# Sums and low parts of activation quarters read from PSUM in the seven-product scheme of a SwiGLU down-projection (one Trainium2 core)

## The chip, the core and the metric

The kernel runs on 1 core of one Trainium2 chip. The metric is the device time of one execution in microseconds (us); times are medians of several executions unless a single profiled execution is named.

## What is computed

The reference is one inference step of a streaming encoder layer: 2048 prompt rows and 64 sample rows, model width 1024. After convolution and attention comes a gated feed-forward part, in which the change lies:

```python
h2 = rms_norm(x, norm2_g) * (1 + sc2) + sh2
gate, up = jnp.split(h2 @ w_ffn_in, 2, axis=-1)         # each 2816 wide
x = x + gt2 * ((jax.nn.silu(gate) * up) @ w_ffn_out)    # 2816 x 1024
```

Everything is float32.

## The kernel before, in words

**Precision.** A float32 product is made of three matmuls (`mm3`): each operand is split into a high part `hi` (type fp32r) and a low part `lo = x - hi`, and TensorE (PE) accumulates hi·hi, hi·lo and lo·hi in PSUM. For activations ScalarE (ACT) writes `hi` with a Copy and VectorE (DVE) or GpSimd (POOL) writes `lo` with a subtraction. For weights ACT writes `whi` and mostly POOL writes `wlo`. Five weight slabs of such parts are held at a time.

**Passes.** The last phase treats the 2112 rows in three passes `s` (`CBLOCKS`: 576, 768 and 768 rows). `half` is half of a pass's rows: 288 in the first, 384 in the other two. The 2816 hidden columns are 22 tiles `f` of 128.

**Gate and up.** `up(f, ...)` makes one hidden tile for both halves by seven products in place of eight (Strassen-Winograd): steps `s2`, `s3`, `s1`, `a12`, `a22`, `a11` of the next tile, and `s4`, each 12 matmuls into a PSUM bank of 384 columns. Banks come from two tags of four banks each: `y` (for the running products `y` and `z`) and `gp` (for `x` and for the down-projection's `pd`). The ends are: `z` times `c1` (silu of the gate, SBUF) is the hidden value of the first half of the rows, and `y` times `v` (SBUF) that of the second half.

**Down, in the second and third pass.** For tiles 4 to 19 (`PAIRS`, eight pairs `f, f+1` per pass, sixteen in all) the down-projection also takes seven products. The two tiles and the two row halves are the four quarters of the left operand: `A11` and `A21` from the even tile, `A12` and `A22` from the odd one. `paired` makes the sums S3 = A11 - A21, S2 = A22 - S3, S1 = S2 + A11 and S4 = A12 - S2, and `put` splits each of the seven operands A11, S3, A12, A22, S2, S1, S4 into `hi` and `lo` in an eighth of the tile `hid`. `low` asks the planner (`either`) whether DVE or POOL does the subtraction.

`down_pair(f, j)` runs while the next pair's `up` is under way, at four points: j=0 (products B21, T3), j=1 (T4, B11), j=2 (T2, T1) and j=3 (B22). Each product is three groups of three matmuls of 512 columns, one group per 128 rows, and after each group DVE adds the bank to a row accumulator in SBUF: `acc<-acc,pd`. Banks are short: T4 goes on in T3's banks, and T2, T1, B22 go on in B11's, so a group of T1 can start only when DVE has added the same bank's T2 group; and with four `gp` banks the last groups of T3 take banks that B21's groups have to leave first.

**Order.** The kernel's text is only one input to the order: the framework that builds the program gives every engine a fixed list of instructions. `Stream` is a planner inside the kernel that keeps a load figure for each engine; it decides which engine makes a low part and when weights are split. In the text, the two SBUF tiles of the pair (`c1`, `v`) receive the hidden values, and all sums and splits read and write SBUF (`paired`, lines 1817 to 1842; `up`, lines 1937 to 1952). S3, S2, S1 and S4 are written over `v`, `v`, `c1` and `c1`.

In the profile nearly all instructions stand under line 104, that of a recording helper, so tiles tell them apart: `hid<-v,hid` and `hid<-s,hid` are low parts of quarters in SBUF, `v<-v` is S2, `v<-s,v` S3, `s<-v,s` S1 and `s<-s,v` S4 (`s` is the buffer that holds `c1`), `wlo<-wst,whi` (or `wup`, `wfo`, `ws`) is the low part of weights.

Of the kernel before, what the change touches and what calls it, by code (L numbers as in the profile page):

```python
# [10 lines left out]
AF = mybir.ActivationFunctionType  # L11
ALU = mybir.AluOpType
# [67 lines left out]
def tile_chunks(lo, hi):  # L80

    tiles = token_tiles(lo, hi)
    t, n = tiles[(len(tiles) + 1) // 2 - 1]
    return [(lo, t + n), (t + n, hi)]
# [499 lines left out]
def streaming_layer(ctx: ExitStack, tc: tile.TileContext, I, O):  # L584
    nc = tc.nc
    stream = Stream()
    pe, dve, act, gps = (
        Meter(e, n, stream) for e, n in ((nc.tensor, "pe"), (nc.vector, "dve"), (nc.scalar, "act"), (nc.gpsimd, "pool"))
    )
# [88 lines left out]
    def split(hi, lo, src):  # L678
        act.activation(hi, src, AF.Copy)
        stream.after("dve", "act")  # L680
        dve.tensor_tensor(lo, src, hi.bitcast(F32), ALU.subtract)

    def either(n, less=0.0):

        d, p = (max(stream.load[e], stream.load["pe"]) for e in ("dve", "pool"))
        return (gps, "pool") if p + 60 + 2.25 * n + less < d + 75 + 1.04 * n else (dve, "dve")

    def low(hi, lo, src, n, less=0.0):
        e, name = either(n, less)
        stream.after(name, "act")  # L690
        e.tensor_tensor(lo, src, hi.bitcast(F32), ALU.subtract)
        return name
# [344 lines left out]
    def half_piece(i, name):  # L1037
        return (wc, wk)[i].tile([P, CW // 2], F32, tag=f"tg{i}", name=name, bufs=2 + i)
# [7 lines left out]
    def load_mixed(c0, c1, i):  # L1046

        src = [[quarter("cin", i) for _ in range(2)] for _ in range(2)]
        for j, a in enumerate((c_d, o_d)):
            for l in range(2):  # L1050
                nc.sync.dma_start(src[l][j][:, :, : c1 - c0].bitcast(F32), a[l, :, :, c0:c1].rearrange("c p t -> p c t"))
        return src
# [437 lines left out]
    for b, stage in ORDER:  # L1490
        lo, hi = PBLOCKS[b]
        if stage == "q":
            free, ahead = {"columns": 0}, {}
# [16 lines left out]
        elif stage == "g":  # L1510
            for g in gates(b, free):
# [3 lines left out]
                if g == SIDE_G and b == len(PBLOCKS) - 1:  # L1515
# [6 lines left out]
                    src = load_mixed(*cs, 0)  # L1522
                    first_gates = gate_columns(*cs, 0)
            norms = ahead
        else:
            if b == 0 and stage == 1:
                bias_rows()
            if stage == 0:
                conv.drain()
                tail.drain()  # L1530
                y = wk.tile([P, 4, YW], F32, tag="y", name="y")
# [33 lines left out]
    def piece(tag, name):  # L1565
        return wk.tile([P, CW // 2], F32, tag=tag, name=name, bufs={"t1": 2, "t2": 3}[tag])
# [117 lines left out]
    c0, c1 = tile_chunks(*CBLOCKS[0])  # L1684
# [3 lines left out]
    for s, (lo, hi) in enumerate(CBLOCKS):  # L1688
        tiles = token_tiles(lo, hi)
        half = (hi - lo) // 2  # L1690
# [58 lines left out]
        def product(ps, w, b, first, last):  # L1749

            for k in range(4):
                mm3(
                    ps[:, :half], w[0][:, k], w[1][:, k], hs[b][0][:, k, :half], hs[b][1][:, k, :half],
                    first and k == 0, last and k == 3, skip_group_check=True,
                )

        def bank(tag):
            return ps_g.tile([P, 512], F32, tag=tag, name="ps", bufs=4)[:, :half]
# [5 lines left out]
        def plus(dst, ps, b):  # L1764
            stream.after("dve", "pe", "act")
            dve.tensor_tensor(dst, ps, b, ALU.add)

        def silu(dst, z):

            tg = half_piece(0, "tg")[:, :half]  # L1770
            stream.after("act", "pe", "dve")
            act.activation(tg, z, AF.Tanh, scale=0.5)
            stream.after("dve", "act")
            dve.scalar_tensor_tensor(dst, tg, 1.0, z, ALU.add, ALU.mult)

        def slot(q):

            return hid[q % 8 // 4][:, q % 4]

        def whole(f, i):  # L1780

            return slot(2 * (f % 2) + i + 4 * (f >= NF - 2))
# [9 lines left out]
        def hidden(f, i, ps):  # L1792
            if s:
                hi, lo = (whole(f, i)[:, j] for j in range(2))
            else:
                hi, lo = (hid[f >= NF - 4 and f % 4 // 2][:, f % 2, j, i * half : (i + 1) * half] for j in range(2))
            stream.after("act", "dve")
            split(hi, lo, ps)

        def plain(f, i, ps):  # L1800
            hidden(f, i, ps)
            yield 1

        quad = {}

        def put(f, name, src):

            q = quad[f - f % 2]
            a = q["parts"][name] = slot(7 * (f // 2 - PAIRS.start // 2) + 4 + len(q["parts"]))
            stream.after("act", "dve")  # L1810
            act.activation(a[:, 0], src, AF.Copy)
            low(a[:, 0], a[:, 1], src, half)

        def minus(dst, x, y, e=ALU.subtract):
            dve.tensor_tensor(dst, x, y, e)

        def paired(f, i, src):

            q = quad.setdefault(f - f % 2, {"parts": {}})
            if f % 2 == 0:  # L1820
                if i == 0:
                    q["a11"] = src
                    put(f, "A11", src)
                else:
                    minus(src, q["a11"], src)
                    q["s3"] = src
                    put(f, "S3", src)
            elif i == 0:
                q["a12"] = src
                put(f, "A12", src)  # L1830
            else:
                put(f, "A22", src)
                yield 1
                s2, s1, s4 = q["s3"], q["a11"], q["a12"]
                minus(s2, src, s2)
                put(f, "S2", s2)
                minus(s1, s2, s1, ALU.add)
                put(f, "S1", s1)
                yield 1
                minus(s4, s4, s2)  # L1840
                put(f, "S4", s4)
            yield 1

        class Operands:
# [18 lines left out]
        begun, late = {}, []  # L1863
# [23 lines left out]
        def rest_of_late(n=99):  # L1887
            while late and n:
                n -= 1
                if next(late[0], None) is None:  # L1890
                    late.pop(0)

        def up(f, ops, at):
            def step(ps, op, b, first, last, e=f):
                product(ps, ops.use(e, op), b, first, last)
                ops.done()

            if f < EARLY:
                s1, c1 = (t[:, :half] for t in early[f])
                y = bank("y")  # L1900
            else:
                y, s1 = begun.pop(f)
                c1 = s1

            z = None
            if not f:
                z = bank("y")
                step(z, "s3", "t3", True, False)
            step(y, "s2", "t2", f < EARLY, False)
            rest_of_late(1)  # L1910
            u2 = piece("t1", "u2")[:, :half]
            keep = (lambda dst, ps: plus(dst, ps, s1)) if f < EARLY else copy
            keep(u2, y)
            if f % 2:
                at(3)
            if f:
                z = bank("y")
                step(z, "s3", "t3", True, False)
            v = half_piece(1, "v")[:, :half]
            keep(v, z)  # L1920
            rest_of_late()
            if f % 2 == 0:
                at(0)
            step(y, "s1", "t1", False, False)
            plus(v, y, v)
            if f % 2:
                at(4)
            if f >= EARLY:
                x = bank("gp")
                step(x, "a12", "b21", True, True)  # L1930
                plus(x, x, s1)
                silu(c1, x)
            if f % 2 == 0:
                at(1)
            step(z, "a22", "t4", False, True)
            plus(z, z, u2)
            two = s and f - f % 2 in PAIRS
            h = [c1, v] if two else [z, y]
            dve.tensor_tensor(h[0], z, c1, ALU.mult)
            if EARLY <= f + 1 < NF:  # L1940
                ny = bank("y")
                step(ny, "a11", "b11", True, False, f + 1)
                begun[f + 1] = ny, piece("t2", "s1")[:, :half]
                copy(begun[f + 1][1], ny)
            for _ in paired(f, 0, h[0]) if two else [hidden(f, 0, z)]:
                pass
            step(y, "s4", "b22", False, True)
            if f < EARLY:
                plus(y, y, s1)
            silu(y, y)  # L1950
            dve.tensor_tensor(h[1], y, v, ALU.mult)
            late.append(paired(f, 1, h[1]) if two else plain(f, 1, y))

        def down(fs, ws):

# [67 lines left out]
        for f in range(0, NF, 2):  # L2023
# [6 lines left out]
            def at(i, f=f):  # L2030
                if s and f - 2 in PAIRS:
                    if i in dn_at(f - 2):
                        down_pair(f - 2, dn_at(f - 2).index(i))
                elif i == 0 and 2 <= f <= NF - 4:
                    down([f - 2, f - 1], [W.get(("fo", e)) for e in (f - 2, f - 1)])
# [10 lines left out]
        for i, (t, n) in enumerate(tiles):  # L2046
            for j in range(2):
                q = 2 * i + j
# [35 lines left out]
```

## Time and profile before

| | |
|---|---|
| median of 3 runs | 3088.68 us (3081.73 to 3092.24) |
| the profiled execution | 3091.31 us, span of its instructions 3089.5 us |
| mean granted TensorE clock | 0.985 |
| PE busy | 2948.6 us (95% of the span) |
| DVE, ACT, POOL busy | 2092.8, 1233.9, 1005.2 us (68%, 40%, 33%) |
| bytes moved by DMA | 693.07 MB, 224 GB/s |

A row of the list of groups gives the operation as out<-in, the count, the busy time and the mean of one in ns, then the idle time of the engine before them and who ended it. A row of the time-ordered list gives start and duration in us; an idle time before it, with the instruction that ended the wait, stands in brackets.

### The profile page before, as it was taken

To read this page: it belongs to the slowest core of one execution; us is meant where nothing else is said; L and a number is where in the kernel's file an instruction comes from. 1 tells how busy PE (TensorE), PEld (TensorE's weight loads), DVE (VectorE), ACT (ScalarE), POOL (GpSimd) and SP (SyncE) were. 2 spreads that over 40 slices of the span, in tenths; PEclk is the share of its full clock that TensorE was granted. 3 is DMA by queue.
4 is the path that set the end of the run, shared out by engine and by line. 5 is a ranking of instruction groups with operands and counts; after the bars stand their busy time and mean duration, and the time that the engine had idled before them with its cause. 6 is when DMAs were issued, how large, how long until landed. Compare 5 with 4: busy or idle time off the path is not lost. (4 is left out here: it accounts for less than half of the span.)

```text
span 3089.5 us, 44838 instructions
## 1 busy us (share of the span) xinstructions
PE 2948.6 (95%) x16259; PEld 2611.9 (85%) x16259; DVE 2092.8 (68%) x3817; ACT 1233.9 (40%) x2212; POOL 1005.2 (33%) x626
## 2 busy tenths in 40 slices
PE   7989898999999999989999999999999999999998
PEld 4789777887888788888888889998888898989887
DVE  4797687777977885466666756556666757366667
ACT  2324431452255257454433345334434244333322
POOL 0200210101011102445666342265766341343341
PEclk9999998999999999999999999999999999999999
DMA  9788788888997798876444776445545955345444
GB/s 341 251 276 304 217 289 275 266 267 267 302 283 234 263 271 248 256 275 223 148 150 141 266 251 216 142 159 180 184 159 195 352 197 191 124 152 176 156 152 175
DMA packets 487082, 693.07 MB, mean 224 GB/s; under 512 B 38484, under 2 KB 316872, under 8 KB 486861
## 3 DMA queue, kind: packets, MB, share of 16 engines
q1 hardware_dynamic: 474581, 672.82, 66.4%
q10 hardware_dynamic: 12280, 17.39, 1.6%
q8 instruction: 128, 2.10, 0.3%
q14 instruction: 93, 0.76, 0.1%
HBM read 505.89 MB, written 184.19 MB: 223 GB/s over the span
## 5 line engine op out<-in xcount | busy, mean ns | idle before, releaser
L104 POOL TENSOR_TENSOR wlo<-wst,whi 128x1024 fp32r<-128x1024 f32 (+1 forms) x175 | 391.6, 2244 | 485.6 <-ACT whi L104 421.5
L104 PE MATMUL ps<-t,whi 128*128 128x384 f32 (+1 forms) x2112 | 503.4, 324 | 11.0 <-DVE t L104 4.8
L104 PE MATMUL pd<-whi,hid 128*128 128x512 f32 (+1 forms) x1400 | 455.1, 394 | 33.4 <-DVE acc L104 33.4
L104 ACT ACTIVATE whi<-wst 128x1024 fp32r<-128x1024 f32 (+1 forms) x269 | 261.8, 977 | 384.6 <-PE ps L104 97.1
L104 PE MATMUL ps<-b,whi 128*128 128x384 f32 (+1 forms) x1584 | 382.6, 327 | 10.8 <-DVE pw L104 4.0
L104 PEld LDWEIGHTS ps<-t,whi 128*128 128x128 f32 x2112 | 370.5, 189 | 20.2 <-DVE t L104 5.8
L104 DVE SCALAR_TENSOR_TENSOR y<-u,wd,y 128x512 f32<-128x512 f32 (+1 forms) x480 | 368.3, 771 | 6.5
L104 PE MATMUL ps<-hh,whi 128*128 128x512 f32 (+2 forms) x992 | 364.1, 367 | 0.0
L104 PE MATMUL ps<-hl,whi 128*128 128x512 f32 (+2 forms) x992 | 347.3, 350 | 0.0
L104 PE MATMUL ps<-hh,wlo 128*128 128x512 f32 (+2 forms) x992 | 346.7, 350 | 0.0
L104 PEld LDWEIGHTS pd<-whi,hid 128*128 128x128 f32 (+1 forms) x1400 | 258.2, 184 | 104.3 <-DVE acc L104 47.0
L104 PE MATMUL ps<-t,wlo 128*128 128x384 f32 (+1 forms) x1056 | 340.6, 323 | 0.0
L104 DVE TENSOR_TENSOR acc<-acc,pd 128x512 f32<-128x512 f32 (+1 forms) x440 | 285.3, 681 | 66.4 <-PE pd L104 62.8
L104 PEld LDWEIGHTS ps<-b,whi 128*128 128x128 f32 x1584 | 279.3, 190 | 14.1 <-DVE pw L104 4.3
L104 PE MATMUL pd<-wlo,hid 128*128 128x512 f32 (+1 forms) x700 | 274.1, 392 | 0.0
L104 PE MATMUL ps<-b,wlo 128*128 128x384 f32 (+1 forms) x792 | 257.9, 326 | 0.0
L104 POOL TENSOR_TENSOR r<-t,mhalf 128x8 f32<-128x8 f32 (+3 forms) x68 | 84.4, 1243 | 392.8 <-DVE t L104 369.4
L104 PEld LDWEIGHTS ps<-hh,wlo 128*128 128x128 f32 x992 | 188.3, 190 | 22.4
L104 PEld LDWEIGHTS ps<-hh,whi 128*128 128x128 f32 x992 | 189.1, 191 | 18.6 <-issue 2.1
L104 PEld LDWEIGHTS ps<-hl,whi 128*128 128x128 f32 x992 | 189.1, 191 | 15.4 <-issue 1.7
L104 POOL TENSOR_TENSOR wlo<-wup,whi 128x1024 fp32r<-128x1024 f32 (+1 forms) x62 | 133.9, 2160 | 208.7 <-ACT whi L104 202.4
L104 PEld LDWEIGHTS ps<-t,wlo 128*128 128x128 f32 x1056 | 199.2, 189 | 0.0
(231 smaller groups left out, 5794.2 us busy)
## 6 DMA issues: line engine op xcount, KB each, us to landing
whi<-w_din_h SPq DMA_DIRECT2D x72, 512.0 KB, 6.4
wlo<-w_din_l SPq DMA_DIRECT2D x72, 512.0 KB, 6.7
wst<-sum_d SPq DMA_DIRECT2D x131, 256.0 KB, 2.9
wmod<-in_w_ada SPq DMA_DIRECT2D x48, 512.0 KB, 8.0
sum_d<-ws SPq DMA_DIRECT2D x88, 256.0 KB, 2.2
wst<-in_w_ffn_in SPq DMA_DIRECT2D x85, 256.0 KB, 3.4
wst<-in_w_ffn_in SPq DMA_DIRECT2D x37, 512.0 KB, 5.3
wst<-in_w_in SPq DMA_DIRECT2D x36, 512.0 KB, 6.6
```

The source lines that it names most:

```text
L104: return f(*args, **kw)
```

## The change

The hidden values stay in their PSUM banks: `z` is overwritten with z·c1 and `y` with y·v. High parts, low parts and sums are taken from there, and the sums are written back into the bank, so each of DVE's subtractions and additions has one operand in PSUM and the other in SBUF. Low parts of quarters are always made by DVE (`split`). Three values that are needed again after their bank is overwritten, or as the second operand of a later sum, are copied to SBUF by ACT: A11 into `c1`, S3 into `v`, and S2 over S3 in `v`.

```diff
-        def put(f, name, src):
+        def put(f, name, ps):
 
             q = quad[f - f % 2]
             a = q["parts"][name] = slot(7 * (f // 2 - PAIRS.start // 2) + 4 + len(q["parts"]))
             stream.after("act", "dve")
-            act.activation(a[:, 0], src, AF.Copy)
-            low(a[:, 0], a[:, 1], src, half)
-
-        def minus(dst, x, y, e=ALU.subtract):
-            dve.tensor_tensor(dst, x, y, e)
-
-        def paired(f, i, src):
+            split(a[:, 0], a[:, 1], ps)
+
+        def paired(f, i, ps, free):
 
             q = quad.setdefault(f - f % 2, {"parts": {}})
-            if f % 2 == 0:
-                if i == 0:
-                    q["a11"] = src
-                    put(f, "A11", src)
-                else:
-                    minus(src, q["a11"], src)
-                    q["s3"] = src
-                    put(f, "S3", src)
+            if f % 2 == 0 and i == 0:
+                put(f, "A11", ps)
+                act.activation(free, ps, AF.Copy)
+                q["a11"] = free
+            elif f % 2 == 0:
+                dve.tensor_tensor(ps, q["a11"], ps, ALU.subtract)
+                put(f, "S3", ps)
+                act.activation(free, ps, AF.Copy)
+                q["s3"] = free
             elif i == 0:
-                q["a12"] = src
-                put(f, "A12", src)
+                put(f, "A12", ps)
+                q["a12"] = ps
             else:
-                put(f, "A22", src)
+                put(f, "A22", ps)
                 yield 1
-                s2, s1, s4 = q["s3"], q["a11"], q["a12"]
-                minus(s2, src, s2)
-                put(f, "S2", s2)
-                minus(s1, s2, s1, ALU.add)
-                put(f, "S1", s1)
+                z, keep = q["a12"], q["s3"]
+                dve.tensor_tensor(ps, ps, keep, ALU.subtract)
+                put(f, "S2", ps)
+                act.activation(keep, ps, AF.Copy)
+                dve.tensor_tensor(ps, ps, q["a11"], ALU.add)
+                put(f, "S1", ps)
                 yield 1
-                minus(s4, s4, s2)
-                put(f, "S4", s4)
+                stream.after("dve", "act")
+                dve.tensor_tensor(z, z, keep, ALU.subtract)
+                put(f, "S4", z)
             yield 1
...
             two = s and f - f % 2 in PAIRS
-            h = [c1, v] if two else [z, y]
-            dve.tensor_tensor(h[0], z, c1, ALU.mult)
+            dve.tensor_tensor(z, z, c1, ALU.mult)
...
-            for _ in paired(f, 0, h[0]) if two else [hidden(f, 0, z)]:
+            for _ in paired(f, 0, z, c1) if two else [hidden(f, 0, z)]:
...
-            dve.tensor_tensor(h[1], y, v, ALU.mult)
-            late.append(paired(f, 1, h[1]) if two else plain(f, 1, y))
+            dve.tensor_tensor(y, y, v, ALU.mult)
+            late.append(paired(f, 1, y, v) if two else plain(f, 1, y))
```

Over the program the change turns 112 low parts (96 on DVE, 16 on POOL) into 112 on DVE, adds 48 ACT copies, and, since the planner's figure for POOL is lower, moves 7 low parts of weights (128x1024) from DVE to POOL, all in the second pass.

What it does to the order is seen at two places of a pair in the second pass. **Place A** is j=2, when T2 and T1 are run: DVE's rows there from the silu of `y` in an even tile on. Before (S3 is `v<-s_21585,v`, its low part `hid<-v,hid`):

```order
L104 SCALAR_TENSOR_TENSOR ps<-tg,ps 128x384
L104 TENSOR_TENSOR v<-ps,v 128x384
L104 TENSOR_TENSOR v<-s_21585,v 128x384
L104 TENSOR_TENSOR acc<-acc,pd 128x512
L104 TENSOR_TENSOR hid<-v,hid 128x384
L104 TENSOR_TENSOR acc<-acc,pd 128x512 x5
L104 TENSOR_TENSOR v<-ps,v 128x384
```

The same place of the changed kernel (S3 is `ps<-s_21593,ps`):

```order
L104 SCALAR_TENSOR_TENSOR ps<-tg,ps 128x384
L104 TENSOR_TENSOR ps<-ps,v 128x384
L104 TENSOR_TENSOR ps<-s_21593,ps 128x384
L104 TENSOR_TENSOR acc<-acc,pd 128x512
L104 TENSOR_TENSOR hid<-ps,hid 128x384
L104 TENSOR_TENSOR acc<-acc,pd 128x512 x5
L104 TENSOR_TENSOR v<-ps,v 128x384
```

Nothing moved here: the same instruction stands between the first and the second addition, with other operands.

**Place B** is j=0, when B21 and T3 are run and S2, S1 and S4 are made, on DVE from the silu of `y` in the odd tile on. Before (`hid<-v,hid` is the low part of A22, then of S2; the low part of S1 is not in DVE's list here, POOL makes it; `hid<-s_21803,hid` is that of S4):

```order
L104 TENSOR_TENSOR v<-ps,v 128x384
L104 TENSOR_TENSOR v<-v 128x384
L104 TENSOR_TENSOR hid<-v,hid 128x384
L104 TENSOR_TENSOR s_21585<-v,s_21585 128x384
L104 TENSOR_TENSOR hid<-v,hid 128x384
L104 TENSOR_TENSOR s_21803<-s_21803,v 128x384
L104 TENSOR_TENSOR acc<-acc,pd 128x512
L104 TENSOR_TENSOR wlo<-wup,whi 128x1024
L104 TENSOR_TENSOR hid<-s_21803,hid 128x384
L104 TENSOR_TENSOR acc<-acc,pd 128x512 x5
L104 TENSOR_TENSOR v<-ps,v 128x384
```

The same place of the changed kernel, in the order low part of A22, S2, two additions, low part of S2, an addition, S1, S4, an addition, low parts of S1 and S4, two additions:

```order
L104 TENSOR_TENSOR ps<-ps,v 128x384
L104 TENSOR_TENSOR hid<-ps,hid 128x384
L104 TENSOR_TENSOR ps<-ps,v 128x384
L104 TENSOR_TENSOR acc<-acc,pd 128x512 x2
L104 TENSOR_TENSOR hid<-ps,hid 128x384
L104 TENSOR_TENSOR acc<-acc,pd 128x512
L104 TENSOR_TENSOR ps<-ps,s_21593 128x384
L104 TENSOR_TENSOR ps<-ps,v 128x384
L104 TENSOR_TENSOR acc<-acc,pd 128x512
L104 TENSOR_TENSOR hid<-ps,hid 128x384 x2
L104 TENSOR_TENSOR acc<-acc,pd 128x512 x2
L104 TENSOR_TENSOR v<-ps,v 128x384
```

Two additions now stand ahead of the rest of the chain where one stood behind it, and the weights' low part is gone from DVE's list. ACT at place B, before (`u` and `v` from `ps` are copies of running products, `hid` the high parts):

```order
L104 ACTIVATE u_22044<-ps 128x384
L104 ACTIVATE hid<-v 128x384 x2
L104 ACTIVATE whi<-wup 128x1024
L104 ACTIVATE v<-ps 128x384
L104 ACTIVATE hid<-s_21585 128x384
L104 ACTIVATE hid<-s_21803 128x384
L104 ACTIVATE whi<-ws 128x512 x2
L104 ACTIVATE whi<-wst 128x1024
```

And in the changed kernel:

```order
L104 ACTIVATE u_22055<-ps 128x384
L104 ACTIVATE hid<-ps 128x384
L104 ACTIVATE whi<-wup 128x1024
L104 ACTIVATE v<-ps 128x384
L104 ACTIVATE hid<-ps 128x384
L104 ACTIVATE v<-ps 128x384
L104 ACTIVATE hid<-ps 128x384
L104 ACTIVATE whi<-ws 128x512
L104 ACTIVATE hid<-ps 128x384
L104 ACTIVATE whi<-ws 128x512
```

The high part of S2 stands behind a weight slab now, the copy of S2 (`v<-ps`, the second) ahead of the high part of S1, and the high part of S4 behind another weight slab.

## The prediction

> **What bounds the kernel now.** PE is busy for 2948.6 of 3089.5 us, so time can only go where PE waits, or be added where it would begin to wait. The change touches the paired stretches of the second and third pass alone, so I first read busy times in those stretches (columns: stretch, length, then busy time and count of PE, PEld, DVE, ACT, POOL, granted clock, DMA share, GB/s), then the list of who PE waits for in them (total, times, longest):
>
> ```profile
> 2060.00:2385.00 325.00, 307.17 (x1596) 283.04 (x1595) 210.69 (x315) 132.37 (x215) 216.66 (x125) 1.00 0.54 179
> 2720.00:3010.00 290.00, 277.79 (x1455) 258.81 (x1455) 182.56 (x281) 95.21 (x153) 116.57 (x51) 1.00 0.48 157
> ...
> PE pd L104 <- DVE acc L104: 17.8, 18, 1.7
> ...
> PE pd L104 <- DVE acc L104: 12.2, 7, 1.7
> ```
>
> PE is idle for 325.00 - 307.17 = 17.8 us in the first stretch and 290.00 - 277.79 = 12.2 us in the second. The waits are the same numbers, in one row each: 25 waits, 30.0 us, all for DVE's addition of a `pd` bank to the accumulator. No wait for weights, for a hidden quarter or for a product's bank is in either answer. So the question is what stands ahead of those additions on DVE. The same operations by tile (minimum/median/maximum ns) show it:
>
> ```profile
> L104 DVE TENSOR_TENSOR hid<-v,hid x48: 544/546/2484, 2032.1 to 3025.5; 128x384 fp32r<-128x384 f32 x48
> L104 DVE TENSOR_TENSOR hid<-s,hid x46: 557/566/1373, 2039.9 to 3028.3; 128x384 fp32r<-128x384 f32 x46
> ...
> L104 DVE TENSOR_TENSOR v<-v x16: 1291/1291/1302, 2044.9 to 3023.4; 128x384 f32<-128x384 f32 x16
> ...
> L104 DVE TENSOR_TENSOR v<-ps,v x98: 445/557/559, 1390.0 to 3054.2; 128x384 f32<-128x384 f32 x76, 128x288 f32<-128x288 f32 x22
> ```
>
> Operations on two SBUF tiles take about 546 ns at best and up to 2484. Those with one operand in PSUM never pass 559, over the whole kernel. What stretches the former is seen at place A, in the third pass (start, duration):
>
> ```profile
> 2770.23 0.56 DVE L104 TENSOR_TENSOR v<-s,v 128x384 f32<-128x384 f32 x1
> 2771.30 0.69 DVE L104 TENSOR_TENSOR acc<-acc,pd 128x512 f32<-128x512 f32 x1 [0.51 <-PE pd L104]
> 2771.93 2.48 DVE L104 TENSOR_TENSOR hid<-v,hid 128x384 fp32r<-128x384 f32 x1
> 2774.34 3.13 DVE L104 TENSOR_TENSOR acc<-acc,pd 128x512 f32<-128x512 f32 x5
> ...
> 2771.62 2.38 POOL L104 TENSOR_TENSOR wlo<-wst,whi 128x1024 fp32r<-128x1024 f32 x1 [1.79 <-ACT whi L104]
> ...
> 2770.42 1.06 ACT L104 ACTIVATE whi<-wst 128x1024 fp32r<-128x1024 f32 x1 [1.42 <-PE ps L104]
> 2771.39 0.51 ACT L104 ACTIVATE hid<-v 128x384 fp32r<-128x384 f32 x1
> ...
> 2772.93 0.39 PE L104 MATMUL pd<-whi,hid 128*128 128x512 f32 x1
> 2775.07 0.50 PE L104 MATMUL pd<-whi,hid 128*128 128x512 f32 x1 [1.75 <-DVE acc L104]
> 2775.41 0.40 PE L104 MATMUL pd<-wlo,hid 128*128 128x512 f32 x1
> 2775.65 0.62 PE L104 MATMUL pd<-whi,hid 128*128 128x512 f32 x2
> ```
>
> S3's low part starts at 2771.93, while POOL's weight subtraction runs until 2774.00, and ends at 2774.41: it lasts until POOL is done and 0.4 us more. Behind it the second addition starts at 2774.34, ends near 2775.0, and PE goes on at 2775.07.
>
> **Step 1, place A (the 7 waits of the third pass and 11 of the second, at 7 places each).** DVE's order there stays; the low part takes S3 from PSUM. The durations of the new forms are in the groups kept apart by shape:
>
> ```profile
> L104 DVE TENSOR_TENSOR hid<-ps,hid 128x384 fp32r<-128x384 f32 x24 | 13.4, 557 | 8.9 <-ACT hid L104 8.2
> L104 DVE TENSOR_TENSOR ps<-ps,s 128x384 f32<-128x384 f32 x38 | 21.5, 566 | 51.2 <-PE ps L104 51.0
> ...
> L104 ACT ACTIVATE hid<-ps 128x384 fp32r<-128x384 f32 x24 | 11.8, 491 | 49.1 <-DVE ps L104 49.1
> L104 ACT ACTIVATE s<-ps 128x384 f32<-128x384 f32 x34 | 16.4, 482 | 6.8 <-PE ps L104 6.8
> ```
>
> ACT's high part starts at 2771.39 as before, behind the same weight slab, and ends at 2771.88. The low part runs from 2771.93 for 0.557, to 2772.49. The second addition then starts at about 2772.5 instead of 2774.34 and ends at 2773.2. The matmul that waits would be asked for 0.23 us after the one at 2772.93, at 2773.16. The 1.75 us wait shrinks to 0 to 0.1 us. The margin is thin: what ACT or DVE loses ahead of this addition, PE waits. The bounds of a residue are 0 and, if S3's high part came later by half a copy (0.24), 0.3 us. I take 0.1, nearer the rows' own reckoning.
>
> [...] The rows have 557 against 546 at best, 11 ns. [...]
>
> **Step 2, place B (the other 7 waits of the second pass).**
>
> ```profile
> 2184.32 0.56 DVE L104 TENSOR_TENSOR v<-ps,v 128x384 f32<-128x384 f32 x1
> 2184.91 1.29 DVE L104 TENSOR_TENSOR v<-v 128x384 f32<-128x384 f32 x1
> ...
> 2188.00 0.67 DVE L104 TENSOR_TENSOR acc<-acc,pd 128x512 f32<-128x512 f32 x1
> 2188.60 1.21 DVE L104 TENSOR_TENSOR wlo<-wup,whi 128x1024 fp32r<-128x1024 f32 x1
> 2189.73 1.37 DVE L104 TENSOR_TENSOR hid<-s,hid 128x384 fp32r<-128x384 f32 x1
> 2191.03 3.06 DVE L104 TENSOR_TENSOR acc<-acc,pd 128x512 f32<-128x512 f32 x5
> ...
> 2183.39 2.40 POOL L104 TENSOR_TENSOR wlo<-wst,whi 128x1024 fp32r<-128x1024 f32 x1 [1.71 <-ACT whi L104]
> 2188.57 2.12 POOL L104 TENSOR_TENSOR hid<-s,hid 128x384 fp32r<-128x384 f32 x1 [2.79 <-ACT hid L104]
> ...
> 2184.45 0.49 ACT L104 ACTIVATE u<-ps 128x384 f32<-128x384 f32 x1 [0.77 <-PE ps L104]
> 2186.66 1.04 ACT L104 ACTIVATE whi<-wup 128x1024 fp32r<-128x1024 f32 x1
> ...
> 2186.33 0.39 PE L104 MATMUL pd<-whi,hid 128*128 128x512 f32 x1
> 2191.76 0.50 PE L104 MATMUL pd<-whi,hid 128*128 128x512 f32 x1 [1.30 <-DVE acc L104]
> ```
>
> S2 lasts until POOL's weights are done (2185.79 and 0.4), three more operations follow, and the second addition stands behind a weight subtraction (1.21) and S4's low part, itself held to 2191.10 by POOL's low part of S1 (until 2190.69). PE waits for that second addition, 1.30 us. In the new order: high part of A22 on ACT 2184.94 to 2185.43, its low part to 2186.0, S2 to 2186.6, and two additions next. The first bank is full after three matmuls from 2186.33, near 2187.2; the additions end at 2187.9 and 2188.5. PE asks at 2191.76 - 1.30 = 2190.46, so 2 us are to spare and the wait is gone.
>
> What is late next: S2's low part now stands behind the slab `whi<-wup` (free to run when PE starts j=0, so until about 2187.5), the ACT copies add 0.48, and S1's low part ends near 2191.9. S4's high part stands behind `whi<-ws`, which needs a slab that PE leaves at the end of j=0, about 2190.5; so S4's low part ends near 2192.4 and the last two additions near 2193.7. Their banks are next written by T4, the product at the start of the stretch below less the 1.4 us saved, from 2195.0. That is hidden.
>
> **Step 3, the rest.** The 48 copies cost 48 x 0.482 = 23 us of ACT, which works 132 of 325 us and 95 of 290: nothing on the path beyond the two places. Sixteen low parts leave POOL (up to 2.12 each) and seven weight parts come (2.4 against 1.24 on DVE, last fence below); at place B one takes the other's slot. PE waits for no weights, and five slabs are held, so I cost this at nothing; uncovered, it would be 7 x 1.2 = 8 us.
>
> **The sum.** All 25 waits are 30.0 us. A matmul after a wait is also slow to restart: 0.34 us from 2775.07 to the next start against 0.24 after it, 25 x 0.1 = 2.5. Less a residue of 0.1 at 14 places A, 1.4. Gain 31.1 us. The profiled execution took 3091.3, which gives 3060.2; against the median of the runs (3088.7, 2.6 lower) it is 3057.6. I predict the middle, 3059.
>
> **Rivals.**
>
> *A wait survives at place A.* For it: the margin is 0.1 us, and S3's high part stands behind a weight slab on ACT. Against: that slab is tied to PE's own progress (1.42 <-PE ps in the row), not to a late load. If 1 us stayed at each of the 14 places, the gain would be 31 - 14 = 17: 3074 against the profiled execution. 12 in 100.
>
> *The stretching stays* because the new forms still have one SBUF operand beside POOL. Against: maximum 559 in 98 instances of `v<-ps,v`. The time would be 3088. 3 in 100.
>
> *Slower: the banks are held too long.* `z` and `y` used to be free after one multiplication; now the odd tile's `y` bank is kept until S1's low part and its `z` bank until S4's. Four `y` banks serve the products in turn, and the first to need that bank is the step `a11` of the tile after next, second of the three steps in this row of the chain (start, duration, kind):
>
> ```profile
> 2200.50 6.34 PE ps L104 x36
> ...
> L104 DVE TENSOR_TENSOR wlo<-wst,whi 128x1024 fp32r<-128x1024 f32 x79 | 98.0, 1243 | 62.4 <-ACT whi L104 59.0 <-DMA bias<-rb_d 2.5 <-DMA out<-acc 0.4
> ```
>
> It starts at 2200.50 + 2.1 = 2202.6, or 2201.2 without the wait. S1's low part ends near 2191.9: 9 us to spare. From there each us that the chain S2, copy, S1 is late costs one us at each of 14 places; slower than now begins at 9 + 2.2 us, as 31 us over 14 places are 2.2. At 13 us late it would be 14 x 4 - 31 = 25 us slower, 3114. Nothing in ACT's rows is that late. 3 in 100.
>
> **How the numbers follow.** Forecast 82 in 100, then 12, 3 and 3. A measurement tells about 0.3%, 9 us, from no change; 3074 is still faster, so faster has 93, same 4 (the second rival and a part of the first), slower 3. The runs before spread from 3082 to 3092. From the fastest less 32.5 (no residue) comes 3049, from the slowest with two thirds of the gain 3071; I widen the low end to 3047 for a slightly faster execution elsewhere and end at 3071, which leaves out most of the first rival.
>
> **What would show it.** In the profile after: PE busy about 98 to 99% of each of the two stretches; the list of PE's waits there empty or some 0.1 us each; `hid<-ps,hid` at 557 throughout with no maximum above 0.6 us; the second addition at place A 0.6 us behind the low part's start; a pair shorter by 17.8 / 7 = 2.5 us (second pass) and 12.2 / 7 = 1.7 us (third). Step 1 is wrong if PE still waits for `acc` at T1's second group, step 2 if at T3's last; step 3 if PE waits for `wlo` or for a `y` bank. The whole is wrong if DVE's operations with a PSUM operand lengthen beside POOL.

## The result and the profile after

The changed kernel takes 3049.25 us (median of 4 runs, 3044.53 to 3052.67) against 3089.06 (4 runs, 3081.73 to 3092.24): a ratio of 0.9873, with a 95% interval of 0.9851 to 0.9895. Two later groups of runs of the kernel before had medians of 3085.7 (13 runs) and 3085.8 us (7 runs), so the gain is 36 to 40 us. The forecast was 3059 us and a gain of 31; the measured time lies near the low end of the range given with it, 3047 to 3071.

The profiled execution of the changed kernel took 3048.72 us, with a span of 3046.9. Its busy times over the whole span are these:

```profile
PE 2936.2 (96%) x16259; PEld 2609.2 (86%) x16259; DVE 2043.0 (67%) x3826; ACT 1254.4 (41%) x2260; POOL 989.7 (32%) x617
```

The same two windows as before (length, then busy time and count of PE, PEld, DVE, ACT and POOL, clock, DMA share, GB/s), a little shifted since the pairs now start earlier:

```profile
2060.00:2385.00 325.00, 325.00 (x1714) 305.57 (x1713) 196.80 (x339) 147.41 (x247) 221.54 (x130) 1.00 0.61 201
2700.00:2990.00 290.00, 290.00 (x1532) 273.02 (x1531) 175.32 (x303) 107.61 (x178) 110.67 (x46) 1.00 0.53 170
```

PE is never idle in them. In the first it now fits 1714 matmuls in 325 us in place of 1596. The low parts from PSUM, by tile (minimum/median/maximum ns):

```profile
L104 DVE TENSOR_TENSOR hid<-ps,hid x180: 443/557/559, 1392.6 to 3021.2; 128x384 fp32r<-128x384 f32 x136, 128x288 fp32r<-128x288 f32 x44
```

Place A in the third pass, the first four rows from DVE's and POOL's part of the time-ordered list, then ACT's, then PE's:

```profile
2740.76 0.69 DVE L104 TENSOR_TENSOR acc<-acc,pd 128x512 f32<-128x512 f32 x1 [0.43 <-PE pd L104]
2741.08 2.42 POOL L104 TENSOR_TENSOR wlo<-wst,whi 128x1024 fp32r<-128x1024 f32 x1 [1.79 <-ACT whi L104]
2741.41 0.56 DVE L104 TENSOR_TENSOR hid<-ps,hid 128x384 fp32r<-128x384 f32 x1
2741.89 3.19 DVE L104 TENSOR_TENSOR acc<-acc,pd 128x512 f32<-128x512 f32 x5
...
2740.91 0.47 ACT L104 ACTIVATE hid<-ps 128x384 fp32r<-128x384 f32 x1
2742.00 0.49 ACT L104 ACTIVATE v<-ps 128x384 f32<-128x384 f32 x1 [0.24 <-DVE hid L104]
...
2742.40 0.39 PE L104 MATMUL pd<-whi,hid 128*128 128x512 f32 x1
2742.63 0.33 PE L104 MATMUL ps<-t,whi 128*128 128x384 f32 x1
2742.80 0.39 PE L104 MATMUL pd<-whi,hid 128*128 128x512 f32 x1
```

The low part takes 0.56 us in the middle of POOL's subtraction (2741.08 to 2743.50), where it took 2.48. The second addition starts 0.48 us behind it, and T1's second group starts at 2742.80 with no wait. Between the groups stands a matmul of the next product, `ps<-t,whi`, that was not there before: PE's own list differs too.

**Where the time went.** Both programs have 16259 matmuls on PE, so the n-th of one can be set against the n-th of the other. The changed kernel gains 5.3 us ahead of the pairs, in code that is the same in both; 22.8 in the second pass's pairs; 0.2 between; 14.05 in the third pass's pairs; nothing behind. The 5.3 belong to the one profiled execution of before: the six other kernels of this study lead it by 2.6 to 7.8 us at that point (counted from the first matmul), five of them with the same code there. The change itself is worth 22.8 + 14.05 = 36.8 us.

That is more than the 30.0 us of waits. Inside a product the matmuls of `pd` start 0.23 us apart and those of `ps` 0.17. Summed over the places where the next start is later than that, the kernel before loses 34.1 us in late starts at 25 places, and 2.7 us (25 x 0.107) in slow restarts: 36.8 us. The changed kernel has no late start over 0.04 us in the pairs.

### The profile page after: what moved, and what is told of

The parts are those of the page before. It is cut to its first block, busy times and chain, and to the rows that moved or that the text cites. A ratio compares the mean times of both kernels' runs of the same rounds, so it can differ in the third digit from the quotient of the medians.

```text
span 3046.9 us, 44878 instructions
## 1 busy us (share of the span) xinstructions
PE 2936.2 (96%) x16259; PEld 2609.2 (86%) x16259; DVE 2043.0 (67%) x3826; ACT 1254.4 (41%) x2260; POOL 989.7 (32%) x617
## 5 line engine op out<-in xcount | busy, mean ns | idle before, releaser
L104 POOL TENSOR_TENSOR wlo<-wst,whi 128x1024 fp32r<-128x1024 f32 (+1 forms) x180 | 402.6, 2243 | 499.5 <-ACT whi L104 427.6
```

The source lines that it names most:

```text
L104: return f(*args, **kw)
```

## The experiments

**Theory one:** PE waited because DVE operations on two SBUF tiles lasted until POOL's subtraction was done; with one operand in PSUM they don't. **Theory two:** the gain comes from the engines' other shares and the new order. The losses below are late starts with their restarts in the pairs of the second and third pass, as above; the waits are the profile's, with their number in brackets. From the loss of e1_dve_lows 1.6 us of a lowered clock are taken out (last section).

| kernel | median us | ratio to before, 95% interval | waits, 2nd / 3rd pass | loss, 2nd / 3rd pass |
|---|---|---|---|---|
| before | 3085.7 to 3089.1 | | 17.8 (18) / 12.2 (7) | 22.7 / 14.1 |
| changed | 3049.25 | 0.9873, 0.9851 to 0.9895 | 0 / 0 | 0 / 0 |
| e1_dve_lows | 3076.51 | 0.9970, 0.9958 to 0.9981 | 9.0 (12) / 12.2 (7) | 12.2 / 14.0 |
| e2_s3_only | 3059.74 | 0.9918, 0.9893 to 0.9942 | 9.2 (7) / 0 | 11.05 / 0 |
| e3_s3_from_sbuf | 3068.66 | 0.9945, 0.9924 to 0.9965 | 4.7 (5) / 12.2 (7) | 6.5 / 14.0 |
| e4_pool_memset | 3060.00 | 0.9915, 0.9895 to 0.9934 | 8.4 (13) / 0 | 12.7 / 0.6 |
| e5_copy_first | 3048.60 | 0.9882, 0.9865 to 0.9898 | 0 / 0 | 0 / 0 |
| e7_low_four_times | 3049.50 | 0.9881, 0.9866 to 0.9895 | 0 / 0 | 0 / 0 |

### The engines' shares alone (e1_dve_lows)

```diff
-            act.activation(a[:, 0], src, AF.Copy)
-            low(a[:, 0], a[:, 1], src, half)
+            split(a[:, 0], a[:, 1], src)
```

in `put` of the kernel before (`split` also makes the copy to the high part), so that DVE always makes the low part.

> The kernel before, with the 112 low parts of quarters always on DVE; all sums and low parts still read two SBUF tiles. This moves the sixteen low parts off POOL and shifts the weights' low parts as the change does, without PSUM operands. Theory one (the waits come from DVE operations with two SBUF operands that last as long as POOL's subtraction): the 14 places A keep their waits, 8.7 us in the second pass and 12.2 us in the third, since the low part of S3 still stretches to about 2 us. At place B the first two additions now stand next to each other in DVE's list, so that the 7 waits of 1.30 us may go by order alone: some 9 to 11 us less than before, about 3078. Theory two (the gain comes from the engines' other shares and the order, not from the operands): nearly the whole gain, about 3050, and no waits at place A.

3076.51 us, 9.2 less than before, as theory one had it. At place A the low part still stretches; third pass, DVE:

```profile
2755.92 0.69 DVE L104 TENSOR_TENSOR acc<-acc,pd 128x512 f32<-128x512 f32 x1 [0.51 <-PE pd L104]
2756.61 2.43 DVE L104 TENSOR_TENSOR hid<-v,hid 128x384 fp32r<-128x384 f32 x1
```

At place B the waits are gone though S2 is still stretched to 1.29. DVE there, in the second pass:

```profile
2175.06 1.29 DVE L104 TENSOR_TENSOR v<-v 128x384 f32<-128x384 f32 x1
...
2178.15 1.27 DVE L104 TENSOR_TENSOR acc<-acc,pd 128x512 f32<-128x512 f32 x2
2179.34 2.04 DVE L104 TENSOR_TENSOR hid<-s,hid 128x384 fp32r<-128x384 f32 x2
```

Two additions stand together ahead of the last low parts, where the second had stood behind a weight subtraction and a low part that POOL's low part of S1 stretched (to 1.37 us); POOL no longer makes that one. The 7 waits at place B, 11.0 us of loss with their restarts, thus go by the engines' other shares and the new order, without any PSUM operand; this run does not tell the two apart.

### S3 alone from PSUM (e2_s3_only)

The kernel before, with this for S3 in `paired`, and S3 formed over `y` in its bank:

```diff
                     minus(src, q["a11"], src)
-                    q["s3"] = src
-                    put(f, "S3", src)
+                    q["s3"] = free
...
+                    split(a[:, 0], a[:, 1], src)
+                    act.activation(free, src, AF.Copy)
```

> The kernel before, with S3 alone formed in PSUM, its low part taken from there on DVE, and copied to SBUF by ACT; A11, A12, A22, S2, S1 and S4 as before. Theory one: the 18 waits at place A, 8.7 + 12.2 us, vanish, the 7 of 1.30 us at place B stay; with about 0.27 us per wait beyond the length shown the time falls by 26 us, to about 3063; with the shown length and 0.1 us, by 23 us. Theory two: no gain, about 3089, as sixteen low parts stay on POOL and the order at place B stays as before.

3059.74 us, 26.0 less than before, against 26 expected. The waits of the second pass's pairs, and PE's busy time in the third's:

```profile
PE pd L104 <- DVE acc L104: 9.2, 7, 1.3
```

```profile
2690.00:3025.00 335.00, 335.00 (x1768) 315.17 (x1767) 206.99 (x343) 114.28 (x186) 133.99 (x59) 1.00 0.52 168
```

All 18 waits at place A are gone and the 7 at place B stand as before. One operand of one quarter in seven carries 25.8 of the 36.8 us (36.8 less 11.05). DVE's list differs from that of before in its operands alone. PE's list has one matmul of the next product ahead of T1's second group at the 14 places A; its 0.17 us are small beside waits of up to 1.75.

### S3 back in SBUF (e3_s3_from_sbuf)

The changed kernel, with

```diff
-                dve.tensor_tensor(ps, q["a11"], ps, ALU.subtract)
-                put(f, "S3", ps)
-                act.activation(free, ps, AF.Copy)
+                dve.tensor_tensor(free, q["a11"], ps, ALU.subtract)
+                put(f, "S3", free)
```

> The changed kernel, with S3 written to SBUF and its high and low parts taken from there; all the rest as in the changed kernel. The low part of S3 is the only one of the seven with two SBUF operands. Theory one: hid<-v stretches to about 2 to 2.5 us beside POOL's weights, and the waits at place A come back, 12 us in the third pass and about 9 in the second; none at place B. Time 22 to 26 us over the changed kernel, about 3073. Theory two: as the changed kernel, about 3049, no waits.

3068.66 us, 19.4 over the changed kernel where 22 to 26 were expected: the third pass's seven waits are back in full, the second pass's at half the size expected, because POOL's subtraction there is further along when the low part starts (by 1.94 us at the short example below, by 0.37 at the long one). That gives different doses of one thing, so the price can be read. A short one (DVE, POOL, PE of the second pass) and a long one (third pass):

```profile
2291.22 0.88 DVE L104 TENSOR_TENSOR hid<-v,hid 128x384 fp32r<-128x384 f32 x1
...
2289.28 2.41 POOL L104 TENSOR_TENSOR wlo<-wup,whi 128x1024 fp32r<-128x1024 f32 x1
...
2292.18 0.39 PE L104 MATMUL pd<-whi,hid 128*128 128x512 f32 x1
2292.76 0.50 PE L104 MATMUL pd<-whi,hid 128*128 128x512 f32 x1 [0.19 <-DVE acc L104]
2293.10 0.39 PE L104 MATMUL pd<-wlo,hid 128*128 128x512 f32 x1
```

```profile
2752.84 2.43 DVE L104 TENSOR_TENSOR hid<-v,hid 128x384 fp32r<-128x384 f32 x1
...
2752.47 2.38 POOL L104 TENSOR_TENSOR wlo<-wst,whi 128x1024 fp32r<-128x1024 f32 x1 [1.79 <-ACT whi L104]
...
2753.79 0.39 PE L104 MATMUL pd<-whi,hid 128*128 128x512 f32 x1
2755.92 0.50 PE L104 MATMUL pd<-whi,hid 128*128 128x512 f32 x1 [1.74 <-DVE acc L104]
2756.26 0.39 PE L104 MATMUL pd<-wlo,hid 128*128 128x512 f32 x1
```

In both the low part ends 0.41 to 0.42 us behind POOL's operation (2291.69 and 2292.10; 2754.85 and 2755.27). PE's starts are 0.58 and 2.13 us apart where 0.23 is usual: 0.35 and 1.90 late, while the list shows waits of 0.19 and 1.74. At all 14 places (low parts of 0.62 to 2.43 us) the late start is the low part's duration less 0.53, to within 0.01. So a wait costs 0.16 us more than its shown length, since that is counted from the modelled end of the matmul ahead (0.39) and not from when the next would have started (0.23), and 0.11 us of restart: the matmul that waited is followed after 0.34 us, not 0.23 (2292.76 to 2293.10, 2755.92 to 2756.26).

### POOL writes, but doesn't read (e4_pool_memset)

The kernel before; DVE's and PE's lists are the same, row for row:

```diff
-            e.tensor_tensor(lo[:, c], src, hi[:, c].bitcast(F32), ALU.subtract)
+            if self.quiet and name == "pool":
+                e.memset(lo[:, c].bitcast(F32), 0.0)
+            else:
+                e.tensor_tensor(lo[:, c], src, hi[:, c].bitcast(F32), ALU.subtract)
```

with `quiet` set in the second and third pass.

> The kernel before, with the low parts of weights that POOL makes in the second and third pass filled with zeros by POOL in place of the subtraction (these low parts are left out of the result). DVE and PE run the lists of before, unchanged; POOL no longer reads two SBUF tiles for the weights. Theory one: hid<-v and v<-v fall to 0.55 us, the waits at place A go (30.0 us of waits fall to 5 at most, what is left being at place B, where POOL still makes the low part of S1), and the time falls by 25 to 35 us to about 3058. Theory two, and any account by the order of DVE or PE: the waits stay, about 3089. If POOL's writes alone hold DVE back, the waits shrink by the share by which POOL's operation gets shorter, and hid<-v still ends 0.4 us behind it.

3060.00 us, 25.7 less than before, with the kernel's own DVE code. S2 by tile, where it had been 1291 throughout:

```profile
L104 DVE TENSOR_TENSOR v<-v x16: 557/557/558, 2037.1 to 2990.6; 128x384 f32<-128x384 f32 x16
```

This leaves theory two no part at place A: no list of DVE, ACT or PE changed, and the 12.2 us of waits in the third pass are gone. By the two traces 23.4 us of the gain lie in the pairs; 3.4 more come ahead of the second pass's pairs and between the passes, where POOL's work is quiet too. The memset was also shorter (0.95 against 2.4 us), and at place A of the third pass it has ended 0.3 us before the low part starts. So that place shows that POOL's subtraction was what held DVE, and not whether its reading or its writing did. On that, 36 operations on two SBUF tiles overlap one of these memsets alone and none takes over 0.56 us; but only eight of them start inside the memset. The other 28 had started before it, and operations that start before a subtraction of POOL are not stretched either (34 of 0.54 to 0.56 us in before, e1_dve_lows and e2_s3_only). I had expected what is left at place B only, 5 us at most; 8.4 are left, six of the thirteen waits at place A of the second pass. There POOL still makes sums of weights (DVE, then POOL):

```profile
2151.51 0.67 DVE L104 TENSOR_TENSOR acc<-acc,pd 128x512 f32<-128x512 f32 x1
2152.18 0.99 DVE L104 TENSOR_TENSOR hid<-v,hid 128x384 fp32r<-128x384 f32 x1
...
2149.86 2.89 POOL L104 TENSOR_TENSOR ws<-wfo,ws 128x512 f32<-128x512 f32 x2
2152.70 0.94 POOL L104 MEMSET wlo<- 128x1024 f32 x1
```

The low part ends at 2153.17, 0.42 us behind the sums (2152.75), in the middle of the memset. At place B the late start falls from 1.47 to 0.83 us. What is left there is not shown to be order, since POOL still makes the low part of S1 and S4's low part is stretched by it, to 1.39 us where it was 1.37 before (DVE, then POOL):

```profile
2175.80 1.22 DVE L104 TENSOR_TENSOR wlo<-wup,whi 128x1024 fp32r<-128x1024 f32 x1
2176.94 1.39 DVE L104 TENSOR_TENSOR hid<-s,hid 128x384 fp32r<-128x384 f32 x1
...
2176.19 1.72 POOL L104 TENSOR_TENSOR hid<-s,hid 128x384 fp32r<-128x384 f32 x1 [4.92 <-ACT hid L104]
```

The low part takes 0.83 us more than 0.56, as much as PE is still late.

### Two attempts to delay the second addition (e5_copy_first, e7_low_four_times)

```diff
                 dve.tensor_tensor(ps, q["a11"], ps, ALU.subtract)
+                act.activation(free, ps, AF.Copy)
                 put(f, "S3", ps)
-                act.activation(free, ps, AF.Copy)
```

> The changed kernel, with ACT's copy of S3 to SBUF ahead of S3's high part instead of behind its low part; nothing else changed. The low part of S3 then starts about 0.48 us later, and with it the second addition at place A. Theory one with the account by starts (a wait costs the whole delay of the matmul's start and 0.11 us of restart): matmuls at each of the 14 places start 0.45 us late, with 0.11 of restart 0.56 each, 8 us in all, about 3057; the list of waits shows only 0.3 each, 4 us. By the shown lengths and 0.1 us each, as the prediction had it, the time would rise by 5.6 us. If the margin at place A were wider than 0.1 us: less than 3 us.

```diff
                 put(f, "S3", ps)
+                for _ in range(3):
+                    dve.tensor_tensor(q["parts"]["S3"][:, 1], ps, q["parts"]["S3"][:, 0].bitcast(F32), ALU.subtract)
                 act.activation(free, ps, AF.Copy)
```

> The changed kernel, with the low part of S3 made four times over at its place in DVE's list (the same values are written each time); this delays the second addition at place A by 3 x 0.48 = 1.45 us without any operation on two SBUF tiles. Theory one: what counts is only how long DVE is kept from the second addition, so PE waits again at all 14 places, 1.45 less the margin of 0.1 and the matmul that stands between, 0.17: 1.2 to 1.3 late at the start and 0.11 of restart, 19 us in all, about 3068; the list of waits shows some 1.1 each, 15 us. If the order of the lists were what counts: no more than 3 us, as the first addition, the low part and the additions behind it stand as in the changed kernel.

Both missed: 3048.60 and 3049.50 us, as the changed kernel. The delay never reached the second addition, since the framework that orders the program answered the edit. DVE at place A, third pass, of the copy ahead and then of the four low parts:

```profile
2740.04 1.38 DVE L104 TENSOR_TENSOR acc<-acc,pd 128x512 f32<-128x512 f32 x2 [0.43 <-PE pd L104]
2741.34 0.55 DVE L104 TENSOR_TENSOR hid<-ps,hid 128x384 fp32r<-128x384 f32 x1
2741.80 2.53 DVE L104 TENSOR_TENSOR acc<-acc,pd 128x512 f32<-128x512 f32 x4
```

```profile
2742.11 0.69 DVE L104 TENSOR_TENSOR acc<-acc,pd 128x512 f32<-128x512 f32 x1 [0.44 <-PE pd L104]
2742.76 0.56 DVE L104 TENSOR_TENSOR hid<-ps,hid 128x384 fp32r<-128x384 f32 x1
2743.23 0.68 DVE L104 TENSOR_TENSOR acc<-acc,pd 128x512 f32<-128x512 f32 x1
2743.82 0.55 DVE L104 TENSOR_TENSOR hid<-ps,hid 128x384 fp32r<-128x384 f32 x1
```

In the first the low part went behind the second addition; in the second one low part went between each two additions. They say nothing on theory one's price, which rests on e3_s3_from_sbuf. They do say that a place between additions is not as scarce as the prediction made it: the framework finds another.

## Why the prediction was right, and what it mis-sized

**The bound** was read rightly: PE's waits for `acc` in the pairs were all that the change could win, and they are what it won.

**Step 1, place A**, held. The row of the low part is 0.56 us beside a running subtraction of POOL (the prediction's "never pass 559" is read from `v<-ps,v`; others with one operand in PSUM take up to 0.567), and e2_s3_only and e3_s3_from_sbuf show that this operand alone takes the waits away and brings them back. The second addition came 0.48 us behind the low part's start (0.6 predicted). The residue of 0.1 us each is what e4_pool_memset shows with PE's list of before: seven slow restarts of 0.09 us in the third pass (0.6 in all), with no late start. In the changed kernel it is 0, because PE's list has the product's matmul, 0.17 us, between T1's first and second group. I had compared DVE's and ACT's lists at place A and not PE's.

The traces tell the two forms apart. Between 2040 and 3025 us of the kernel before, e1_dve_lows and e2_s3_only, 160 of DVE's 128x384 operations on two SBUF tiles started inside a subtraction or sum of POOL: every one ended 0.41 to 0.42 us behind it. In these three and the changed kernel 499 with one operand in PSUM did: 0.55 to 0.57 us each. For a POOL operation that only writes the evidence is thinner: the eight that started inside a memset of e4_pool_memset took 0.55 to 0.56 us each.

**Step 2, place B**, had the right result, and its reasons can now be weighed. The prediction named the stretched S2 and the new order together. Other shares of the engines and the new order are enough without a PSUM operand, with S2 still at 1.29 us (e1_dve_lows). With the order of before, S2 at 0.56 and S4's low part still stretched, 0.83 us of 1.47 are left (e4_pool_memset). No run takes all of the stretching at place B away in the order of before, so whether that would be enough too stays open. So of the 36.8 us, 25.8 at place A come from the PSUM operand of S3, and 11.0 at place B can be had without one.

**Step 3** held: ACT is busy 20.5 us longer (23 estimated), and PE waits neither for `wlo` nor for a bank of `y` in the pairs.

**The sum** is where the size was off: 31.1 predicted, 36.8 measured. The term that failed is the cost of a wait, which I took as the shown length and 0.1 us of restart. The late starts are 34.1 us for 30.0 us of shown waits, 4.1 more (25 x 0.16); the restarts 2.7 for 2.5; the residue 0 for 1.4. Together 5.7. The rest of the miss in the predicted time is its base: from the later medians of before, 3085.7, less 36.8 comes 3048.9, where the profiled execution of before gave 3054.5. That execution spent some 5 us more ahead of the pairs, in code that did not change. That the time still fell inside the range is in part luck: its low end, 3049 before it was widened, is the fastest run of before less all waits at the price that was too small.

**The rivals** did not come. No wait survived at place A, though the margin was as thin as said: carried on below its shortest low part (0.62 us), the line of e3_s3_from_sbuf gives a late PE from 0.53 us on, an estimate, and the low part takes 0.557; the 0.17 us of the pulled matmul cover it. The stretching did not stay, by the 499 above. Banks held too long would show as waits of PE for `ps`; there are none in the pairs.

## What to carry to other kernels

When an operation of DVE has a median of 0.55 us and a maximum of 2.5, look at what POOL does at that instant: here two SBUF operands made the difference, and moving one of them to PSUM freed DVE (0.56 us in place of 2.48 for the low part of S3) without giving POOL less to do. It paid only where such an operation stood ahead of something that PE waited for (in e1_dve_lows S2 was still stretched to 1.29 us and no wait was left at place B); of seven quarters one carried 70% of the gain, and the rest could be had by other shares of the engines and another order. Take the price of a PE wait from the distance of matmul starts and not from the list of waits alone, and compare the lists of all engines before calling an order unchanged.

## What the runs showed of the hardware

In e3_s3_from_sbuf a wait of PE cost 0.27 us more than its shown length, whether it was shown as 0.2 or 1.7 us long: 0.16 by which the row of the matmul ahead (0.39 us, to its modelled end) runs past the next usual start (0.23), and 0.11 of restart (0.34 us to the next start and not 0.23).

One longer wait cost more. In e1_dve_lows a low part of 2.74 us at one place of the second pass made PE wait 2.05 us. Its rows, and three windows (before the wait ended, the next 3.1 us, and behind), where the last three columns are clock, DMA share and GB/s:

```profile
2202.31 0.50 PE L104 MATMUL pd<-whi,hid 128*128 128x512 f32 x1 [2.05 <-DVE acc L104]
2202.65 0.44 PE L104 MATMUL pd<-wlo,hid 128*128 128x512 f32 x1
2202.88 1.05 PE L104 MATMUL pd<-whi,hid 128*128 128x512 f32 x2
2203.73 0.63 PE L104 MATMUL pd<-wlo,hid 128*128 128x512 f32 x1
```

```profile
2200.00:2202.50 2.50, 0.45 (x3) 0.19 (x2) 2.50 (x3) 0.00 (x0) 2.50 (x2) 1.00 0.03 9
2202.90:2206.00 3.10, 3.10 (x10) 2.71 (x9) 1.92 (x3) 1.06 (x1) 3.02 (x3) 0.50 0.48 144
2206.10:2208.00 1.90, 1.90 (x12) 1.90 (x12) 0.00 (x0) 0.35 (x1) 1.90 (x2) 0.95 0.00 0
```

The granted clock fell to 0.50 for some 3.4 us, which cost 1.6 us more. None of the waits of 1.74 to 1.75 us, 21 in three kernels' third passes, was followed by this. In the pairs it is one instance, but the traces hold more outside them. In every kernel but e4_pool_memset PE waits 2.37 to 2.43 us once ahead of the second pass's pairs and once between the passes (in before until 1939.2 and 2596.3 us), and a stretch of 3.4 us at clock 0.50 stands beside each; in e4_pool_memset the longest wait there is 1.0 us and the clock stays. The length of the wait alone does not decide it: the wait of 2.05 us above was followed by it, while the changed kernel waits 1.98 us until 862.4 and 2.16 us until 1204.4, and the clock stays at 1.00 behind both.
